# Four small loads from GpSimd to ScalarE's queue, and seven products in the first wide block

## The chip, the cores and the metric

The kernel runs on one core of a Trainium2 chip. The core's engines work side by side, each through its own queue in order: TensorE (PE: matmuls, with PEld its weight loads), VectorE (DVE), ScalarE (ACT), GpSimd (POOL) and SyncE (SP), which here only issues transfers. Three of them issue DMAs: SyncE, ScalarE and GpSimd. The metric is the time on the device in microseconds (us), lower is better.

## What is computed

One layer of a decoder for 256 positions of width 2048, all in float32: a norm, one large projection of 17408 columns, windowed attention in three groups of heads, a gated linear recurrence, gates, a mixing projection, and a gated feed-forward part. The change lies in the first blocks of the projection and in the loads beside them:

```
a = rmsnorm(h, norm_mix_pre[layer])
proj = a @ w_in[layer]
q_a, k_a, v_a, q_r, f_r, i_r, g_r, gate_a, gate_r = split_columns(proj)
...
qh = rotary(heads(q_a), S)                                  # cs: the rotary table
lower_bounds = cumsum(softmax(hgrn_lower_bounds, axis=0), axis=0)
r_out = r_out * hgrn_norm_gain[layer] ... * silu(g_r)       # gainr
y = sigmoid(gate_a) * (attn @ w_attn_branch[layer]) + sigmoid(gate_r) * (r_out @ w_hgrn_branch[layer])
...
a = rmsnorm(h, norm_ffn_pre[layer])
```

## The kernel before

Each float32 matrix is split into a rounded high part and the rest, and a product is made of three matmuls (high x high, high x low, low x high). The split of a weight tile is one copy on ScalarE (the high part, L293 or L328) and one subtraction on VectorE (the rest, L294 or L330).

The weights come in blocks. A block has a number of steps, and each step loads a tile `raw`, splits it and multiplies it. Tiles are loaded about three units ahead (`N_RAW`), splits are written two steps ahead of their matmuls (`AHEAD`), and the split tiles rotate through three buffers (`N_SPLIT`). The order of the work on each engine is the order in which the program writes it; the main loop at the end writes, for each step, the split of the step after next, the load behind that, the step's matmuls, and a piece of whatever stands in the lists `evacs`, `turns` and `lanes`.

The kernel begins with two "N" blocks of eight steps (columns `COL_GR`, the gate of the recurrence, 512 columns each), which accumulate in four banks called `acc`. While the first of them runs, TensorE transposes x (`transpose_in`, L492), ScalarE and VectorE store the transposed x with its high and low parts (L499, L503), and ScalarE squares x for the norm (`sumsq`, L570). A generator `opening` writes these squares, one per step, and behind them the scale of the norm, its broadcast, the rotary tables (`cs`) and the bounds of the recurrence (`rowg`). Between the fourth and the fifth square it writes four loads on GpSimd's queue: `gainr` (the norm's gain broadcast to 128 partitions, 512 KB), two times 16 rows of `rowg` (8 KB each) and `cs` (256 KB). GpSimd has nothing ahead of them but a few fills. When an "N" block is done, `evac_g` empties its two banks: a sigmoid on ScalarE (L747), two products on VectorE (L749 reads the bank, L752 multiplies by `gainr`), and a store.

Behind them stand eight wide blocks (`early`), each 1024 columns in two groups of 512, in eight steps of 256 rows. A plain step multiplies a 2 x 2 arrangement of tiles with eight products, 24 matmuls; its split is L328 and L330. A step "by seven" makes the same contribution with seven products of sums of tiles, 21 matmuls; its split makes sums first (VectorE L334, L340, L341), then high parts (ScalarE L339, L342, L345) and the rest (VectorE L346, L348). It needs sums of the tiles of xT too, which `pair_sums` makes ahead (`x7`, the tiles `so`). The results of a wide block lie in four banks for the pairs (side, group), and the products by seven use four more, `p1`, `p6`, `p5` and `p7`, which `gather` adds behind the last step by seven and `evac_kept` adds to the first four. One kind of bank is called `aux`, the other `acc`; blocks take turns. In the first wide block the pairs lie in `aux`.

The order of a wide block's steps is a list of pairs (tile of rows, by seven or not):

```
FIRST = [(m, 0) for m in range(8)]
EIGHT = [(3, 0), (4, 0), (0, 1), (5, 0), (1, 1), (6, 0), (2, 1), (7, 0)]
```

`FIRST` is used for the first wide block, `EIGHT` for all others. The second wide block begins with a flush of `lanes[1]`, which writes what is left of `pair_sums`. A flush of `evacs` comes behind the second step of each wide block (`turn=1`); in the first wide block it writes what is left of `evac_g` of the second "N" block.

Of the kernel before, what the change touches and what calls it, by code (L numbers as in the profile page):

```python
# [19 lines left out]
P = 128  # L20
# [6 lines left out]
HW = 1024  # L27
# [6 lines left out]
COL_GA, COL_GB = 13312, 15360  # L34

X7 = H7 = (0, 1, 2)
FIRST = [(m, 0) for m in range(8)]
EIGHT = [(3, 0), (4, 0), (0, 1), (5, 0), (1, 1), (6, 0), (2, 1), (7, 0)]
DOWN = [[(m, m in by7) for m in range(KF // 2)] for by7 in (range(4, 20, 3), range(3, 19, 3))]

# [50 lines left out]
def tile_hybrid_block(ctx: ExitStack, tc: tile.TileContext, t, out):  # L91
    nc = tc.nc
# [20 lines left out]
    def hslot(s):  # L113
        return hpool.tile([P, 2, 512], F32, tag="h", bufs=4, name=nm(s))

    def aux():
        return auxp.tile([P, 512], F32, tag="aux", name=nm("aux"))
# [10 lines left out]
    def small(s, n=8, bufs=6):  # L128
        return cpool.tile([P, n], F32, tag=f"small{n}", bufs=bufs, name=nm(s))
# [4 lines left out]
    def rsqrt_mean(dst, ss, n, bias=None):  # L134

        w = ss.shape[-1]
        v, y, a = (small(s)[:, :w] for s in ("v", "y", "a"))  # L140
        bias = bias or (eps[:, 0:1], eps[:, 1:2])
        nc.scalar.activation(y, ss, AF.Ln, scale=1.0 / n, bias=bias[0])
        nc.scalar.activation(y, y, AF.Exp, scale=-0.5)
        nc.vector.tensor_scalar(v, ss, -0.5 / n, bias[1], op0=OP.mult, op1=OP.add)
        if w == 1:
            nc.vector.scalar_tensor_tensor(out=a, in0=y, scalar=v, in1=y, op0=OP.mult, op1=OP.mult)
        else:
            nc.vector.tensor_mul(a, y, y)
            nc.vector.tensor_mul(a, a, v)
        nc.vector.scalar_tensor_tensor(  # L150
            out=dst, in0=a, scalar=1.5, in1=y, op0=OP.add, op1=OP.mult
        )
# [11 lines left out]
    rowg = cpool.tile([48, P], F32, name="rowg")  # L164
# [30 lines left out]
    def ptile(s):  # L195
        n = {"early": 4, "middle": 5, "late": 2}[pool["name"]]
        return pool["now"].tile([P, 512], F32, tag="p", bufs=n, name=nm(s))

    cs = kp.tile([P, 2, S], F32, name="cs")
    amask = kp.tile([P, 2, 512], F32, name="amask")  # L200
    lmask = kp.tile([P, len(LEVELS), 64], F32, name="lmask")
    gainr = kp.tile([P, HW], F32, name="gainr")
# [16 lines left out]
    def add_seven(*args, flip, **kw):  # L219
        b = Wide(*args, **kw)  # L220
        b.flip = flip
        blocks.append(b)
        for i in range(b.steps):
            seq.append(Step(b, i, len(units), 0))
            units.append([seq[-1]])
# [286 lines left out]
    def row_broadcast(dst, rc):  # L512

        ds = [small("diag", P, 2) for _ in range(2)]
        for b in range(2):
            nc.vector.tensor_scalar(ds[b], ident, rc[:, b : b + 1], None, op0=OP.mult)
        yield
        ps = aux()
        for b in range(2):
            mm(ps[:, b * P : (b + 1) * P], ones[:, :P], ds[b], True, True)  # L520
        yield
        nc.scalar.activation(dst, ps[:, :S], AF.Copy)
# [12 lines left out]
    evacs, turns, lanes, work, done = deque(), deque(), [deque(), deque()], deque(), []  # L535
    ready = set()

    def advance(q):
        if q:
            try:  # L540
                next(q[0])
            except StopIteration:
                q.popleft()
                return
# [7 lines left out]
    def flush(q):  # L552
        while q:
            advance(q)


    xt = [hslot("x") for _ in range(4)]
# [3 lines left out]
    xT = Split("xT", KD)  # L561
# [4 lines left out]
    def sumsq(dst, pieces, first=0):  # L566
        for j, x in enumerate(pieces, first):
            for b in range(2):
                junk = ptile("junk")
                nc.scalar.activation(  # L570
                    junk, x[:, b, :], AF.Square, accum_out=dst[:, 4 * b + j : 4 * b + j + 1]
                )
                yield

    def add_parts(dst, ss):
        nc.vector.tensor_reduce(
            dst, ss.rearrange("p (b j) -> p b j", b=2), op=OP.add, axis=mybir.AxisListType.X
        )

    def opening():  # L580
        ss, s2 = small("ss"), small("s2")
        yield from sumsq(ss, xt[:2])
        nc.gpsimd.dma_start(gainr, t["hgrn_norm_gain"].to_broadcast([P, HW]))
        nc.gpsimd.dma_start(rowg[0:16], t["norm_ffn_pre"][0].rearrange("(a p) -> a p", p=P))
        nc.gpsimd.dma_start(
            rowg[16:32], t["hgrn_lower_bounds"].rearrange("l (a p) -> (l a) p", p=P)
        )
        nc.gpsimd.dma_start(cs, t["rope"])
        yield from sumsq(ss, xt[2:], 2)
        add_parts(s2[:, :2], ss)  # L590
        rsqrt_mean(r1c, s2[:, :2], D)
        ready.add("r1c")
        yield from row_broadcast(rowb, r1c)
        ready.add("rowb")
        yield
        for i, (j, c) in enumerate(((0, -QSCALE), (1, -QSCALE), (0, 1.0), (1, 1.0))):
            nc.vector.scalar_tensor_tensor(
                out=tabs[:, i, :].rearrange("p (two j) -> p two j", two=2),
                in0=cs[:, j, :].rearrange("p (j two) -> p two j", two=2), scalar=c,
                in1=rowb.rearrange("p (two j) -> p two j", two=2), op0=OP.mult, op1=OP.mult,  # L600
            )
        yield
        ps = aux()
        nc.tensor.transpose(ps[:, :32], rowg[:32], ident[:32, :32])
        yield
        nc.vector.tensor_copy(colg[:, 16:48], ps[:, :32])
        l0, l1 = colg[:, 32:40], colg[:, 40:48]
        m, e0, e1 = small("m"), small("e0"), small("e1")
        nc.vector.tensor_max(m, l0, l1)
        nc.vector.tensor_sub(e0, l0, m)  # L610
        nc.vector.tensor_sub(e1, l1, m)
        nc.scalar.activation(e0, e0, AF.Exp)
        nc.scalar.activation(e1, e1, AF.Exp)
        nc.vector.tensor_add(e1, e0, e1)
        nc.vector.reciprocal(e1, e1)
        nc.vector.tensor_mul(lb, e0, e1)
        nc.vector.tensor_scalar(lb1, lb, -1.0, 1.0, op0=OP.mult, op1=OP.add)
        ready.add("lb")
        yield
        nc.sync.dma_start(amask, t["amask"])  # L620
        nc.sync.dma_start(lmask, t["lmask"])
# [7 lines left out]
    def start():  # L629
        keep_warm(WARM)  # L630
        ps = aux()
        nc.tensor.transpose(ps[:, :16], rowg[:16], ident[:16, :16])
        nc.vector.tensor_copy(colg[:, :16], ps[:, :16])
        high, low = transpose_in(xt, colg, xT, 0, True)
        for kk in range(2):
            high(kk)
            low(kk)
            split(seq[0], kk)
        keep_warm(BRIDGE - 1)
        split(seq[1])  # L640
        lanes[0].append(opening())

    x7 = {}
# [20 lines left out]
    def evac_kept(key, fn):  # L664
        def go(b):
            dst = keep(key, 1024)
            for s, g in ((0, 0), (0, 1), (1, 0), (1, 1)):
                src = b.bank[s, g]
                if b.rest:
                    e = b.rest[s, g]  # L670
                    nc.vector.tensor_add(e, src, e)
                    src = e
                else:
                    e = eslot()
                nc.scalar.activation(e, src, fn, scale=r1c[:, s : s + 1])
                nc.scalar.dma_start(dst[:, s, g * 512 : (g + 1) * 512], e)
            yield
        return go
# [596 lines left out]
    w_in = t["w_in"][0]  # L1275
# [19 lines left out]
             (COL_GA + 1024, ("a", 1), AF.Sigmoid), (COL_GB + 1024, ("r", 1), AF.Sigmoid)]  # L1295
    early += [(COL_V + 1024 * g, ("v", g), AF.Copy) for g in range(3)] + [(COL_IR, "i", AF.Copy)]
    for n, (col, key, fn) in enumerate(early):
        add_seven(w_in, (col, col + 512), EIGHT if n else FIRST, xT, lambda m: x7[m],
                  evac_kept(key, fn), flip=n % 2 == 1, turn=1,
                  pre=(lambda: flush(lanes[1])) if n == 1 else None)  # L1300
    for half in range(2):
        add_wide(w_in, KD, COL_FR + 512 * half, xT, evac_f(half))
        if half == 0:
# [15 lines left out]
    for j in range(4):  # L1319
        add("N", t["w_mix_out"][0], KD, 512 * j, lambda k: yT[0].after(turns)(k), evac_mix(j),  # L1320
            pre=begin_mix if j == 0 else None)
# [3 lines left out]
        pre=begin_ffn, mid=mid_ffn, post=more_h)  # L1325
    add("N", w, KD, FF, lambda k: hT[0](k), evac_first_up)
    for j in range(1, 11):
        add_seven(w, (512 * j, FF + 512 * j), EIGHT, lambda k: hT[0](k),
                  lambda m: h7[m], evac_ffn, flip=j % 2 == 0, turn=1,
                  pre=(lambda: (flush(evacs), flush(lanes[1]))) if j == 1 else None)  # L1330
    for j in range(2):
        add_seven(t["w_ffn_down"][0], (1024 * j, 1024 * j + 512), DOWN[j], act,
                  lambda m: a7[m], evac_down, prep=prep_act, flip=j == 1,
                  pre=begin_down if j == 0 else None, turn=3 if j == 0 else None)
# [45 lines left out]
    a, b, c = seq[-3:]  # L1380
# [61 lines left out]
```

## Time and profile before

| | us |
|---|---|
| median of three runs | 1722.15 |
| lowest, highest | 1721.54, 1722.41 |
| the profiled execution | 1722.01 |
| its span in the trace | 1720.2 |
| TensorE busy | 1704.2 |
| VectorE busy | 1356.5 |
| ScalarE busy | 895.5 |

Times in the trace count from the start of the span. A row of the timeline has start, length, engine, line, operation, tiles and count; the brackets at its end show how long the engine was idle ahead of it and what ended that. A row of a stretch has for each engine the busy time with the number of instructions, then the granted clock of TensorE, the busy share of the 16 DMA engines, and GB/s. A matmul's length in the trace overlaps the next one's; their pace is read from a row with many of them.

### The profile page before, as it was taken

How to read it: one execution, taken by the hardware profiler on the slowest of the kernel's cores; microseconds unless marked ns; L12 is line 12 of the kernel's file. 1: busy time of each engine (PE TensorE's matmuls, PEld its weight loads, DVE VectorE, ACT ScalarE, POOL GpSimd, SP SyncE). 2: the span in 40 equal slices, each digit the busy share in tenths (PEclk: the TensorE clock that was granted, in tenths of full speed). 3: DMA queues.
4: the chain of work that ended last, by engine and by line, in shares of the span. 5: the costliest groups of instructions: out<-in, count | busy, mean ns of one | idle time of the engine just before them, and what ended most of it. 6: DMA issues, size and time to landing. Idle time of an engine off the chain costs nothing.

```text
span 1720.2 us, 21535 instructions
## 1 busy us (share of the span) xinstructions
PE 1704.2 (99%) x8356; PEld 1431.0 (83%) x8356; DVE 1356.5 (79%) x1477; ACT 895.5 (52%) x1007; POOL 23.7 (1%) x42
## 2 busy tenths in 40 slices
PE   8999999999999999999999999999999999999997
PEld 6888888888888898888888878888888888888886
DVE  5768888886677887777665578888888888898998
ACT  5645555554434434544444466555555555665663
POOL 0000000000000000000000000000000000000000
PEclk9999999999999999999999999999999999999999
DMA  6865666667554655465555745555555555656653
GB/s 241 277 220 209 234 232 226 220 220 257 175 167 160 218 162 172 163 208 168 171 172 188 253 165 202 196 195 196 198 201 202 202 201 200 219 198 215 201 198 115
DMA packets 208678, 344.78 MB, mean 200 GB/s; under 512 B 10960, under 2 KB 77696, under 8 KB 208576
## 3 DMA queue, kind: packets, MB, share of 16 engines
q1 hardware_dynamic: 198496, 318.61, 54.9%
q10 hardware_dynamic: 6880, 13.51, 2.1%
q0 software_dynamic: 3200, 11.29, 2.0%
q8 instruction: 65, 1.06, 0.3%
q14 instruction: 37, 0.30, 0.1%
HBM read 331.83 MB, written 11.53 MB: 200 GB/s over the span
## 4 chain that ended last, share of the span: by engine, by line
PE 97%; DMA 1%; DVE 1%; ACT 0%; SPq 0%; issue 0%; DVEq 0%; ACTq 0%
PE acc L132 63%; PE aux L132 33%; DMA raw<-in_w_in 1%; PE aux L819 0%; DMA gpost<-in_norm_mix_post 0%; PE aux L492 0%; PE acc L1133 0%; DVE fz L1262 0%; PE aux L1133 0%; PE aux L480 0%; ACT junk L1216 0%; DVE e L1212 0%; SPq L564 0%; PE aux L967 0%; SPq L272 0%
## 5 line engine op out<-in xcount | busy, mean ns | idle before, releaser
L294 DVE TENSOR_TENSOR w<-raw,w 128x1024 fp32r<-128x1024 f32 (+1 forms) x225 | 274.2, 1219 | 192.7 <-ACT w L293 192.0
L293 ACT ACTIVATE w<-raw 128x1024 fp32r<-128x1024 f32 (+1 forms) x225 | 236.9, 1054 | 297.3 <-PE acc L132 246.3
L132 PE MATMUL acc<-xT,w 128*128 128x256 f32 (+1 forms) x2048 | 370.4, 339 | 0.0
L132 PEld LDWEIGHTS acc<-xT,w 128*128 128x128 f32 x2048 | 311.6, 188 | 43.3
L330 DVE TENSOR_TENSOR wl<-raw,w 128x2048 fp32r<-128x2048 f32 x125 | 285.9, 2287 | 60.9 <-ACT w L328 60.9
L328 ACT ACTIVATE w<-raw 128x2048 fp32r<-128x2048 f32 x125 | 238.8, 1910 | 132.5 <-PE aux L132 64.2
L346 DVE TENSOR_TENSOR wl<-sum,w 128x2048 fp32r<-128x2048 f32 x63 | 144.3, 2291 | 65.6 <-ACT w L342 65.5
L132 PE MATMUL acc<-w,hT 128*128 128x512 f32 x622 | 181.5, 391 | 0.3 <-ACT hT L499 0.3
L132 PE MATMUL acc<-w,xT 128*128 128x512 f32 x536 | 158.4, 397 | 3.5 <-ACT xT L499 1.9
L339 ACT ACTIVATE w<-sum 128x1024 fp32r<-128x1024 f32 x63 | 67.0, 1063 | 172.5 <-DVE sum L334 153.7
L132 PEld LDWEIGHTS acc<-w,hT 128*128 128x128 f32 x622 | 115.9, 188 | 24.7 <-ACT hT L499 0.5
L132 PE MATMUL aux<-w,hT 128*128 128x512 f32 x430 | 135.6, 389 | 0.0
L132 PEld LDWEIGHTS acc<-w,xT 128*128 128x128 f32 x536 | 101.3, 191 | 26.5 <-ACT xT L499 2.1
L132 PE MATMUL aux<-w,xT 128*128 128x512 f32 x386 | 120.9, 389 | 0.0
L348 DVE TENSOR_TENSOR dl<-raw,dh 128x1536 fp32r<-128x1536 f32 x63 | 110.4, 1752 | 0.0
L132 PEld LDWEIGHTS aux<-w,hT 128*128 128x128 f32 x430 | 80.7, 188 | 16.8
L345 ACT ACTIVATE dh<-raw 128x1536 fp32r<-128x1536 f32 x63 | 92.9, 1474 | 0.0
L132 PE MATMUL acc<-w,yT 128*128 128x512 f32 x384 | 88.2, 390 | 0.1
L132 PEld LDWEIGHTS aux<-w,xT 128*128 128x128 f32 x386 | 72.5, 188 | 15.0
L132 PEld LDWEIGHTS acc<-w,yT 128*128 128x128 f32 x384 | 71.8, 188 | 15.3 <-DVE w L294 0.5
L132 PE MATMUL aux<-wl,hT 128*128 128x512 f32 x215 | 83.6, 389 | 0.0
L132 PE MATMUL acc<-wl,hT 128*128 128x512 f32 x215 | 83.6, 389 | 0.0
(262 smaller groups left out, 2653.9 us busy)
## 6 DMA issues: line engine op xcount, KB each, us to landing
raw<-in_w_in SPq DMA_DIRECT2D x271, 512.0 KB, 4.6
raw<-in_w_ffn_gate_up SPq DMA_DIRECT2D x176, 512.0 KB, 4.4
raw<-in_w_ffn_down SPq DMA_DIRECT2D x88, 512.0 KB, 4.8
raw<-in_w_mix_out SPq DMA_DIRECT2D x32, 512.0 KB, 4.9
kept<-e ACTq DMA_DIRECT2D x32, 256.0 KB, 4.4
raw<-in_w_hgrn_branch SPq DMA_DIRECT2D x16, 512.0 KB, 4.5
raw<-in_w_attn_branch SPq DMA_DIRECT2D x16, 512.0 KB, 4.6
v<-kept POOLq DMA_DIRECT2D x8, 512.0 KB, 6.6
```

Of the source, the lines that this page charges most:

```text
L132: nc.tensor.matmul(ps, lhsT, rhs, start=start, stop=stop, skip_group_check=True)
L293: nc.scalar.activation(wh[:, k], raw[:, k], AF.Copy)
L294: nc.vector.tensor_sub(wl[:, k], raw[:, k], wh[:, k].bitcast(F32))
L328: nc.scalar.activation(hi, raw, AF.Copy)
L330: nc.vector.tensor_sub(lo, raw, hi.bitcast(F32))
L339: nc.scalar.activation(hi[:, :1024], s[:, :1024], AF.Copy)
L345: nc.scalar.activation(dhi, d, AF.Copy)
L346: nc.vector.tensor_sub(lo, s, hi.bitcast(F32))
L348: nc.vector.tensor_sub(dlo, d, dhi.bitcast(F32))
```

## The change

The four loads are written on ScalarE's queue, behind six squares instead of four. The first wide block takes the list `EIGHT` as the others do, so that its third, fifth and seventh steps go by seven, and it gathers; the flush of `lanes[1]` moves from the second wide block to the first. One line falls away, so the lines of the changed kernel are one lower.

```diff
-FIRST = [(m, 0) for m in range(8)]
 EIGHT = [(3, 0), (4, 0), (0, 1), (5, 0), (1, 1), (6, 0), (2, 1), (7, 0)]
...
         ss, s2 = small("ss"), small("s2")
-        yield from sumsq(ss, xt[:2])
-        nc.gpsimd.dma_start(gainr, t["hgrn_norm_gain"].to_broadcast([P, HW]))
-        nc.gpsimd.dma_start(rowg[0:16], t["norm_ffn_pre"][0].rearrange("(a p) -> a p", p=P))
-        nc.gpsimd.dma_start(
+        yield from sumsq(ss, xt[:3])
+        nc.scalar.dma_start(gainr, t["hgrn_norm_gain"].to_broadcast([P, HW]))
+        nc.scalar.dma_start(rowg[0:16], t["norm_ffn_pre"][0].rearrange("(a p) -> a p", p=P))
+        nc.scalar.dma_start(
             rowg[16:32], t["hgrn_lower_bounds"].rearrange("l (a p) -> (l a) p", p=P)
         )
-        nc.gpsimd.dma_start(cs, t["rope"])
-        yield from sumsq(ss, xt[2:], 2)
+        nc.scalar.dma_start(cs, t["rope"])
+        yield from sumsq(ss, xt[3:], 3)
...
-        add_seven(w_in, (col, col + 512), EIGHT if n else FIRST, xT, lambda m: x7[m],
+        add_seven(w_in, (col, col + 512), EIGHT, xT, lambda m: x7[m],
                   evac_kept(key, fn), flip=n % 2 == 1, turn=1,
-                  pre=(lambda: flush(lanes[1])) if n == 1 else None)
+                  pre=(lambda: flush(lanes[1])) if n == 0 else None)
```

The order on the engines: on ScalarE, in the eighth step of the first "N" block, where `w` is a split weight tile, `x` and `junk` belong to the squares:

```order
L570 ACTIVATE junk_356,ss_213<-x_112 128x512
L293 ACTIVATE w_358<-raw_179 128x1024 [waits DMAHW7_49,DVE_49]
L570 ACTIVATE junk_375,ss_213<-x_113 128x512 [waits DMAHW4_49]
L293 ACTIVATE w_385<-raw_179 128x1024 [waits DMAHW0_49,DVE_49,PE_49]
L570 ACTIVATE junk_401,ss_213<-x_113 128x512 [waits Activation_49]
L411 ACTIVATE so_379<-s_380 128x512 [waits DVE_49]
```

With the change:

```order
L569 ACTIVATE junk_352,ss_213<-x_112 128x512
L292 ACTIVATE w_354<-raw_179 128x1024 [waits DMAHW7_49,DVE_49]
L582 DMA gainr<-in_hgrn_norm_gain 128x1024
L583 DMA rowg<-in_norm_ffn_pre 16x128
L584 DMA rowg<-in_hgrn_lower_bounds 16x128
L587 DMA cs<-in_rope 128x512 [waits DMAHW0_49]
L569 ACTIVATE junk_375,ss_213<-x_113 128x512 [waits DMAHW4_49]
L292 ACTIVATE w_385<-raw_179 128x1024 [waits DVE_49,PE_49]
```

The four loads have moved between the sixth and the seventh square, and the last of them waits for an earlier DMA (DMAHW0 is one of the counters of completed transfers). On VectorE, at the splits for the first wide block (`wl` is the rest of a weight tile, `sig` the gate in work, `g` its result):

```order
L330 TENSOR_TENSOR wl_596<-raw_472,w_595 128x2048
L413 TENSOR_TENSOR so_567<-s_568,so_567 128x512
L330 TENSOR_TENSOR wl_616<-raw_517,w_615 128x2048
L330 TENSOR_TENSOR wl_655<-raw_577,w_654 128x2048
L749 SCALAR_TENSOR_TENSOR sig_652<-acc_410,r1c,sig_652 128x512
L752 TENSOR_TENSOR g_650<-sig_652,gainr 128x512
```

With the change:

```order
L329 TENSOR_TENSOR wl_596<-raw_472,w_595 128x2048
L412 TENSOR_TENSOR so_567<-s_568,so_567 128x512
L333 TENSOR_TENSOR sum_617<-raw_517 128x1024
L339 TENSOR_TENSOR sum_617<-raw_517,sum_617 128x512
L340 TENSOR_TENSOR sum_617<-raw_517,sum_617 128x512
L345 TENSOR_TENSOR wl_616<-sum_617,w_615 128x2048
L347 TENSOR_TENSOR dl_624<-raw_517,dh_623 128x1536
L329 TENSOR_TENSOR wl_664<-raw_577,w_663 128x2048
L748 SCALAR_TENSOR_TENSOR sig_661<-acc_410,r1c,sig_661 128x512
L751 TENSOR_TENSOR g_659<-sig_661,gainr 128x512
```

Five instructions stand in the place of one, ahead of the reading of the bank `acc_410`.

On TensorE, in the third step of the first wide block, before (the first of its four banks, `aux_622`, and the start of the second; `w` and `wl` are the two parts of the weights):

```order
L132 MATMUL aux_622<-w_615,xT_116 128x512 [waits Activation_49]
L132 MATMUL aux_622<-wl_616,xT_116 128x512 [waits DVE_49]
L132 MATMUL aux_622<-w_615,xT_116 128x512 x2
L132 MATMUL aux_622<-wl_616,xT_116 128x512
L132 MATMUL aux_622<-w_615,xT_116 128x512
L132 MATMUL aux_629<-w_615,xT_116 128x512
```

With the change, the products `p6`, `p5` and `p7`, which have three matmuls each in banks of the kind `acc`:

```order
L131 MATMUL acc_728<-w_615,so_379 128x512
L131 MATMUL acc_728<-wl_616,so_379 128x512
L131 MATMUL acc_728<-w_615,so_379 128x512
L131 MATMUL acc_732<-w_615,so_379 128x512 [waits DVE_49]
L131 MATMUL acc_732<-wl_616,so_379 128x512
L131 MATMUL acc_732<-w_615,so_379 128x512
L131 MATMUL acc_736<-w_615,so_379 128x512 [waits DVE_49]
L131 MATMUL acc_736<-wl_616,so_379 128x512
L131 MATMUL acc_736<-w_615,so_379 128x512
```

The step has taken on banks that the second "N" block used, and waits for VectorE ahead of two of them.

## Prediction

> **What bounds the kernel now.** I read the page first, then stretches of the opening by engine, then the timeline and the chain of waits up to the end of the first wide block.
>
> ```profile
> PE 1704.2 (99%) x8356; PEld 1431.0 (83%) x8356; DVE 1356.5 (79%) x1477; ACT 895.5 (52%) x1007; POOL 23.7 (1%) x42
> PE 97%; DMA 1%; DVE 1%; ACT 0%; SPq 0%; issue 0%; DVEq 0%; ACTq 0%
> ```
>
> TensorE carries 97% of the chain that ended last. So a change counts where TensorE waits, where its clock is low, or by the matmuls that it takes away. The waits lie in the opening, and so does a slow clock:
>
> ```profile
> core 0: us, PE busy (x) PEld busy (x) DVE busy (x) ACT busy (x) POOL busy (x), PEclk, DMA share, GB/s
> 2.00:4.00 2.00, 2.00 (x6) 0.76 (x5) 0.00 (x0) 0.46 (x1) 0.24 (x1) 1.00 0.87 243
> 4.00:6.50 2.50, 2.50 (x13) 1.20 (x11) 0.91 (x3) 1.27 (x3) 1.37 (x3) 1.00 0.92 270
> 7.81:11.23 3.42, 2.15 (x10) 1.61 (x11) 0.69 (x1) 0.87 (x2) 0.00 (x0) 1.00 1.05 386
> 11.23:14.64 3.41, 1.55 (x8) 0.81 (x7) 1.23 (x1) 1.05 (x2) 0.00 (x0) 1.00 1.04 390
> 14.64:18.06 3.42, 2.11 (x4) 1.29 (x5) 2.56 (x5) 3.42 (x8) 0.00 (x0) 0.50 1.05 386
> 18.06:21.47 3.41, 3.41 (x9) 2.58 (x9) 1.46 (x2) 0.42 (x1) 0.00 (x0) 0.50 1.05 386
> 21.47:24.90 3.43, 3.43 (x19) 2.78 (x18) 1.15 (x3) 2.40 (x5) 0.00 (x0) 1.00 1.05 385
> ```
>
> The DMA engines are full (share 1.04 to 1.06) while TensorE is idle for half of 11.23 to 14.64. Behind that idle stretch the granted clock is 0.50 for 6.83 us. The chain there, in order of time (start, length, what):
>
> ```profile
> 4.57 9.82 DMA raw<-in_w_in
> 14.41 1.06 ACT w L293
> 17.18 4.54 PE acc L132 x10
> 22.15 2.78 PE acc L132 x12
> 63.07 43.80 PE aux L132 x192
> ```
>
> A weight load issued at 4.57 lands at 14.39; ScalarE, in order, splits it (L293) before it can take xT (L499), and only then TensorE goes on. The last row is the first wide block: TensorE without a gap. The same place in the timeline (start, length, what, and in brackets the idle time ahead and what ended it):
>
> ```profile
> 1.55 0.69 POOL L583 DMA_DIRECT2D gainr<-in_hgrn_norm_gain  x1
> 6.12 0.57 POOL L588 DMA_DIRECT2D cs<-in_rope  x1
> 8.18 0.63 ACT L293 ACTIVATE w<-raw 128x512 fp32r<-128x512 f32 x1 [1.59 <-DMA raw<-in_w_in]
> 10.51 1.64 PE L132 MATMUL acc<-w,xT 128*128 128x512 f32 x6
> 13.38 0.63 PE L492 MATMUL aux<-ident,x 128*128 128x128 f32 x4 [1.23 <-DMA x<-in_x]
> 15.88 5.83 PE L132 MATMUL acc<-w,xT 128*128 128x512 f32 x12 [1.88 <-ACT xT L499]
> ```
>
> TensorE ends the first step at 12.15 and has only four transposes (0.63) to do before it resumes at 15.88. ScalarE waited for weights already at 8.18.
>
> **The four loads leave the opening: gain.** GpSimd issues gainr (512 KB), two loads of 8 KB and cs (256 KB) between 1.55 and 6.69 us, into the full stretch. Up to the landing at 14.39 the queues moved (packets, MB, share; q0 is GpSimd's, q1 SyncE's), and from 4.0 to 6.5 (last two rows):
>
> ```profile
> q1 hardware_dynamic: 1929, 3.18, 63.8%
> q0 software_dynamic: 288, 0.80, 17.9%
> ...
> q0 software_dynamic: 131, 0.50, 70.6%
> q1 hardware_dynamic: 103, 0.17, 21.2%
> ```
>
> Lower bound: 0.80 MB less at 0.390 MB per us is 2.05 us. Upper bound: from 4.0 to 6.5 the engines moved only 270 GB/s, most of it gainr; if q1 alone ran at 388 from 4.0 on, its remaining 2.7 MB (3.18 less the 2 us at 243 before) would be in at 10.95, 3.4 us earlier. I take 3.0, nearer the upper end, since the slow stretch coincides with gainr's packets. The resumption follows the landing: 15.88 becomes 12.9.
>
> The clock adds to that. The first step ends at 12.15 now because the second half of its weights is split at 8.18; ScalarE is free for that 1.59 earlier, so the step would end near 10.6. The gap to 12.9 holds 0.6 us of transposes, so 1.7 us are idle. In 3.41 us that leaves 1.7 busy, between the 1.55 after which the clock fell and the 2.15 after which it did not. I take it that the clock holds (about 2 in 3). Then the ten matmuls of 4.54 us take 10 x 2.78 / 12 = 2.3: 2.2 us less. Gain of the opening: 3.0 + 2.2 = 5.2 us; bounds 2.05 and 5.6.
>
> **ScalarE issues them: nothing, while covered.** On ScalarE's queue (the order above) the issues stand ahead of the last two squares, behind a weight split. What such issues cost on this queue, and what waits there:
>
> ```profile
> 36.33 1.05 ACT L293 ACTIVATE w<-raw 128x1024 fp32r<-128x1024 f32 x1
> 37.28 0.62 ACT L570 ACTIVATE junk<-x 128x512 f32<-128x512 f32 x1
> 40.34 0.63 ACT L411 ACTIVATE so<-s 128x512 fp32r<-128x512 f32 x1 [0.78 <-DVE s L409]
> 50.21 0.69 DVE L752 TENSOR_TENSOR g<-sig,gainr 128x512 f32<-128x512 f32 x1
> ...
> 940.23 3.24 ACTq L1017 DMA_DIRECT2D hx<-in_x  x4
> ...
> 1480.83 0.83 ACTq L1185 DMA_DIRECT2D fpost<-in_norm_ffn_post  x2
> ```
>
> fpost is a broadcast like gainr, 0.41 us each, and starts while the ACTIVATE ahead of it runs. Four take 1.65 from 36.34 on, so the square moves from 37.28 to 38.0. That 0.7 vanishes in the 0.78 for which L411 waits on VectorE anyway. At hx's 0.81 each (3.24) the delay would be 2.3, 1.5 past the cover, on VectorE's path; four 128- and 16-row transfers are nearer fpost. cs's issue waits (DMAHW0 in the order) for an earlier DMA of SyncE, the weights that the split after the square needs landed in any case. GpSimd's queue loses four issues and next waits for g at 50 us. Nothing waits for the data: gainr is first read at 50.21, over 10 us behind the issue, and SyncE's weight loads of 30 to 40 us do not fill the engines.
>
> **The first wide block: 9 matmuls less, 3.3 us of waits more.** A step has 24 matmuls, by seven products 21. At 43.80 / 192 = 0.228 us, three such steps save 2.05. Against that stands VectorE's order: the long split of step 2 (steps counted from 0; L333 to L347 with the change) now stands ahead of L748, which empties the bank acc_410, and TensorE's order shows that the fifth product (acc_732) and the seventh (acc_736) wait for VectorE, since they take over the two banks of the second "N" block.
>
> Durations, VectorE first: the next block's split by seven products, then what stands there now; ScalarE behind it.
>
> ```profile
> 66.30 2.29 DVE L330 TENSOR_TENSOR wl<-raw,w 128x2048 fp32r<-128x2048 f32 x1
> 72.98 0.75 DVE L749 SCALAR_TENSOR_TENSOR sig<-acc,r1c,sig 128x512 f32<-128x512 f32 x1
> 75.15 0.69 DVE L752 TENSOR_TENSOR g<-sig,gainr 128x512 f32<-128x512 f32 x1
> ...
> 116.51 1.22 DVE L334 TENSOR_TENSOR sum<-raw 128x1024 f32<-128x1024 f32 x1
> 122.52 1.76 DVE L348 TENSOR_TENSOR dl<-raw,dh 128x1536 fp32r<-128x1536 f32 x1
> ```
>
> ```profile
> 65.35 1.28 ACT L747 ACT_TABLE_LOAD   x1
> 66.65 0.69 ACT L747 ACTIVATE sig<-acc,r1c 128x512 f32<-128x512 f32 x1
> 74.27 1.92 ACT L328 ACTIVATE w<-raw 128x2048 fp32r<-128x2048 f32 x1 [2.95 <-PE aux L132]
> ...
> 120.18 1.47 ACT L345 ACTIVATE dh<-raw 128x1536 fp32r<-128x1536 f32 x1
> ```
>
> Such a split takes 124.28 - 116.51 = 7.77 us. In today's times (the gain of the opening shifts everything alike, since these engines follow TensorE's steps up to 35 us): it runs 66.3 to 74.07, and TensorE, done with step 1 at 74.2 (the release of L328), starts step 2 unhindered. ScalarE: L345 until 71.4, table 72.7, sigmoid 73.3, L328 of step 3 until 75.2. VectorE: L330 until 77.5, then the first bank at 78.2; the second at 79.55. The fifth product comes at 74.2 + 12 x 0.228 = 76.9 and waits 1.3; the seventh waits another 0.65. Step 2 ends at 80.95, step 3 at 86.4. Step 4's split starts when both gates are done (72.98 to 75.84 is 2.86), at 80.2, and ends at 87.97; its second matmul, due at 86.6, waits 1.35. Step 6's split begins at 90.2 and ends at 97.95, when TensorE arrives: no wait. Together 3.3 - 2.05 = 1.25 us longer. This end hangs on VectorE alone; were the banks free and the splits early, it would be 2.05 shorter.
>
> The steps' weights come in another order, in loads of the same size, and the flush moved to this block finds only work that stood in the same place (L412). The gather and four additions behind the block cost VectorE more, but the second block carries them today without a wait of TensorE.
>
> **Sum.** 1722.01 (the profiled execution; the median is 0.14 above) - 5.2 + 1.25 = 1718.1.
>
> **Rivals.** (1) The clock falls again. The gap is close to the one that made it fall; then only the landing counts: 1722.0 - 3.0 + 1.25 = 1720.3, or 1721.2 with 2.05. The Trainium skill (TensorE: Matmul & The Clock Gate, the HAM clock gate) says the windows of 3.4 us run freely, so that the loss varies between executions of one kernel. That agrees with 6.83 us here being two windows; one execution can't show the varying. (2) The block doesn't wait: 1722.0 - 5.2 - 2.05 = 1714.8. Against it stands the order above. (3) Slower: the opening gains nothing, because q1's pace is set by something other than q0, and ScalarE's issues cost hx's price: 1722.0 + 1.25 + 1.5 = 1724.8; it is slower than before once the opening gives under 1.25 us (2.75 with the dear issues). The 21.2% against 70.6% speaks against it. By the Trainium skill (DMA: Bandwidth & Descriptors, Rules for kernel authors) spreading DMAs over issuing engines doesn't help, as all share 16 engines; by that alone the opening gives 0. The trace agrees on the sharing, but here the time of issue moves too.
>
> **Numbers.** Forecast 0.50, rival (1) 0.25, (2) 0.13, (3) 0.08, other 0.04. A measurement of this kernel tells some 0.2% (3.4 us) from no change, so the borders are 1718.7 and 1725.6. The forecast's own range, 1716.8 to 1719.7 (landing 2.05 to 3.4, block 0.8 to 2), lies two thirds below 1718.7: 0.34; with (2), 0.01 of (1) and half of the others, faster has 0.50. Same has 0.44: 0.16 of the forecast, 0.24 of (1), half of (3). Slower by over 0.2% has 0.06: the other half of (3), which 1724.8 lies close to, and half of the others. The range from 1715.0 to 1721.9 leaves out half of (2) and all of (3).
>
> **What would show it.** Right: no q0 before 14 us, the weight load of 4.57 landing at 11 to 12, clock 1.00 to 21 us, the second step's ten matmuls in 2.3 us; in the first wide block waits of TensorE of about 1.3 and 0.65 in step 2 and 1.35 in step 4. Wrong: a stretch of clock 0.50 behind the opening, L411 later against the transposes than now, or no wait for L748's banks.

## The result, and the profile after

| us | before | after |
|---|---|---|
| median of 20 executions each | 1721.49 | 1720.43 |
| lowest, highest | 1720.95, 1722.89 | 1718.82, 1722.49 |
| the profiled execution | 1722.01 | 1718.82 |
| its span | 1720.2 | 1717.0 |

The ratio is 0.9992, interval 0.9985 to 0.9999: faster by 0.08%, inside the 0.2% that count as no change. The profiled execution of after is the lowest of its twenty, and it gained 3.2 us, three times what the medians gained. So two questions stand: do the parts of the sum show in this profile, and what do the other executions lose again?

The profile's busy times of after (engine, us, share, instructions): TensorE has the nine instructions less.

```profile
PE 1700.6 (99%) x8347; PEld 1428.2 (83%) x8347; DVE 1373.6 (80%) x1497; ACT 900.3 (52%) x1014; POOL 21.7 (1%) x38
```

The chain of waits of after (start, length, what):

```profile
4.38 7.17 DMA raw<-in_w_in
...
14.34 2.60 PE acc L131 x10
17.38 2.78 PE acc L131 x12
...
97.67 6.12 PE aux L131 x27
103.79 12.24 PE acc L131 x54
```

The load lands at 11.55 instead of 14.39, 2.84 earlier. The ten matmuls take 2.60 instead of 4.54, and the step behind them starts at 17.38 instead of 22.15: the opening gained 4.77. The first wide block ends at 103.79; before, at 63.07 + 43.80 = 106.87. So 3.08 of the 4.77 are left, and the block itself became 1.69 longer.

The opening by stretches, in the columns of the table shown of before (the last three numbers are the granted clock, the DMA share and GB/s):

```profile
4.00:6.50 2.50, 2.50 (x10) 1.37 (x9) 0.51 (x2) 0.84 (x2) 0.00 (x0) 1.00 0.89 262
11.23:14.64 3.41, 1.23 (x5) 0.59 (x4) 1.97 (x4) 3.06 (x8) 0.00 (x0) 1.00 1.05 387
14.64:18.06 3.42, 3.42 (x18) 2.78 (x17) 2.05 (x4) 1.66 (x4) 0.00 (x0) 1.00 1.05 386
18.06:21.47 3.41, 3.41 (x19) 2.79 (x18) 2.10 (x3) 2.59 (x7) 0.00 (x0) 1.00 1.06 389
```

The clock is 1.00 throughout. From 4.0 to 6.5 the DMA engines moved 262 GB/s without GpSimd's loads, 270 with them; what changed is whose bytes they are, SyncE's alone now:

```profile
q1 hardware_dynamic: 477, 0.65, 89.2%
```

0.65 MB against 0.17. ScalarE's timeline around the four issues (its queue is ACTq):

```profile
30.32 0.36 ACTq L582 DMA_DIRECT2D gainr<-in_hgrn_norm_gain  x1
30.71 0.46 ACTq L583 DMA_DIRECT2D rowg<-in_norm_ffn_pre  x1
31.20 0.44 ACTq L584 DMA_DIRECT2D rowg<-in_hgrn_lower_bounds  x1
31.68 0.43 ACTq L587 DMA_DIRECT2D cs<-in_rope  x1
32.53 0.62 ACT L569 ACTIVATE junk<-x 128x512 f32<-128x512 f32 x1
35.58 0.63 ACT L410 ACTIVATE so<-s 128x512 fp32r<-128x512 f32 x1 [0.78 <-DVE s L408]
```

The square stands at 32.53 where 37.28 less 4.77 puts it, and the 0.78 that L410 waits for VectorE is untouched. Nothing was pushed back.

In the first wide block, TensorE and VectorE in the timeline:

```profile
71.79 0.39 PE L131 MATMUL acc<-w,so 128*128 128x512 f32 x1
73.52 0.50 PE L131 MATMUL acc<-w,so 128*128 128x512 f32 x1 [1.35 <-DVE sig L748]
73.86 0.40 PE L131 MATMUL acc<-wl,so 128*128 128x512 f32 x1
74.10 0.39 PE L131 MATMUL acc<-w,so 128*128 128x512 f32 x1
74.91 0.50 PE L131 MATMUL acc<-w,so 128*128 128x512 f32 x1 [0.43 <-DVE sig L748]
75.25 0.39 PE L131 MATMUL acc<-wl,so 128*128 128x512 f32 x1
...
81.85 0.39 PE L131 MATMUL aux<-dh,xT 128*128 128x512 f32 x1
83.32 0.50 PE L131 MATMUL aux<-dl,xT 128*128 128x512 f32 x1 [1.08 <-DVE dl L347]
83.65 0.39 PE L131 MATMUL aux<-dh,xT 128*128 128x512 f32 x1
```

```profile
70.52 2.29 DVE L329 TENSOR_TENSOR wl<-raw,w 128x2048 fp32r<-128x2048 f32 x1 [1.22 <-ACT w L327]
72.73 0.74 DVE L748 SCALAR_TENSOR_TENSOR sig<-acc,r1c,sig 128x512 f32<-128x512 f32 x1
74.11 0.74 DVE L748 SCALAR_TENSOR_TENSOR sig<-acc,r1c,sig 128x512 f32<-128x512 f32 x1
75.50 1.22 DVE L333 TENSOR_TENSOR sum<-raw 128x1024 f32<-128x1024 f32 x1
81.51 1.75 DVE L347 TENSOR_TENSOR dl<-raw,dh 128x1536 fp32r<-128x1536 f32 x1
```

TensorE waits three times where the block had no gap: twice for the banks that L748 empties, once for step 4's `dl`. The clock stays at 1.00 behind the banks here:

```profile
76.00:79.50 3.50, 3.50 (x17) 2.90 (x16) 2.30 (x4) 2.35 (x3) 1.14 (x2) 1.00 0.94 311
```

The executions of after, sorted by the mean granted clock listed with each: eight at 0.999 took 1718.82 to 1719.61 us, ten at 0.996 to 0.998 took 1720.34 to 1721.06, two at 0.995 took 1722.28 and 1722.49. A stretch of 3.41 us at half clock (half of the 6.83 us seen in the profile of before) lowers the mean over 1717 us by 3.41 x 0.5 / 1717 = 0.001 and costs up to 1.7 us of matmuls. By the times, then, the ten look as if they had one such stretch more and the two as if they had two. The means alone would allow one to four; they are rounded, and they also count the end of the kernel, where no matmul runs (clock 0.61 from 1712 to 1715 us in the profile of after). Theory: the parts of the sum came as in the profile, and the clock, kept there, falls in most executions. Rivals: the block's waits alone cost more than the profile shows, or the loads gain less.

### The profile page after: what moved, and what is told of

Read it like the earlier page. It is cut to its first block, busy times and chain, and to the rows that moved or that the text cites. A ratio compares the mean times of both kernels' runs of the same rounds, so it can differ in the third digit from the quotient of the medians.

```text
span 1717.0 us, 21554 instructions
## 1 busy us (share of the span) xinstructions
PE 1700.6 (99%) x8347; PEld 1428.2 (83%) x8347; DVE 1373.6 (80%) x1497; ACT 900.3 (52%) x1014; POOL 21.7 (1%) x38
## 3 DMA queue, kind: packets, MB, share of 16 engines
q8 instruction: 65, 1.06, 0.3%
## 4 chain that ended last, share of the span: by engine, by line
PE 94%; DVE 3%; ACT 1%; DMA 1%; issue 1%; SPq 0%; ACTq 0%; DVEq 0%
PE acc L131 62%; PE aux L131 31%; DVE w L293 1%; DMA raw<-in_w_in 0%; PE aux L818 0%; DMA gpost<-in_norm_mix_post 0%; PE aux L491 0%; PE acc L1132 0%; DVE fz L1261 0%; PE aux L1132 0%; ACT w L327 0%; PE aux L479 0%; ACT junk L1215 0%; ACT w L292 0%; DVE sig L748 0%
## 5 line engine op out<-in xcount | busy, mean ns | idle before, releaser
L329 DVE TENSOR_TENSOR wl<-raw,w 128x2048 fp32r<-128x2048 f32 x122 | 279.0, 2286 | 41.6 <-ACT w L327 41.5
L327 ACT ACTIVATE w<-raw 128x2048 fp32r<-128x2048 f32 x122 | 232.9, 1909 | 110.1 <-PE aux L131 43.9
L345 DVE TENSOR_TENSOR wl<-sum,w 128x2048 fp32r<-128x2048 f32 x66 | 151.2, 2291 | 68.9 <-ACT w L341 68.8
L347 DVE TENSOR_TENSOR dl<-raw,dh 128x1536 fp32r<-128x1536 f32 x66 | 115.6, 1751 | 0.0
L131 PE MATMUL aux<-w,xT 128*128 128x512 f32 x344 | 108.5, 389 | 0.0
L344 ACT ACTIVATE dh<-raw 128x1536 fp32r<-128x1536 f32 x66 | 97.3, 1474 | 0.0
L131 PE MATMUL acc<-w,a 128*128 128x512 f32 x268 | 83.7, 389 | 0.0
```

The lines of the kernel that those rows point to most:

```text
L131: nc.tensor.matmul(ps, lhsT, rhs, start=start, stop=stop, skip_group_check=True)
L327: nc.scalar.activation(hi, raw, AF.Copy)
L329: nc.vector.tensor_sub(lo, raw, hi.bitcast(F32))
L344: nc.scalar.activation(dhi, d, AF.Copy)
L345: nc.vector.tensor_sub(lo, s, hi.bitcast(F32))
L347: nc.vector.tensor_sub(dlo, d, dhi.bitcast(F32))
```

## The experiments

Before was run again beside each of the three batches of experiments, with medians of 1721.54 us (the loads alone, the block alone and the two first bridges), 1721.36 (steps 3 and 5 with and without the bridge, the loads late on GpSimd, the banks first) and 1721.26 (the rest). A difference between versions of different batches carries these 0.3 us. Behind each median stand in brackets the lowest and the highest execution, then the ratio to before and its 95% interval.

**The loads alone.** The first wide block stays as before.

```diff
+FIRST = [(m, 0) for m in range(8)]
...
-        add_seven(w_in, (col, col + 512), EIGHT, xT, lambda m: x7[m],
+        add_seven(w_in, (col, col + 512), EIGHT if n else FIRST, xT, lambda m: x7[m],
                   evac_kept(key, fn), flip=n % 2 == 1, turn=1,
-                  pre=(lambda: flush(lanes[1])) if n == 0 else None)
+                  pre=(lambda: flush(lanes[1])) if n == 1 else None)
```

> The change's loads alone: four loads on ScalarE behind six squares, the first wide block plain as before. Theory (the opening gives some 4.8 us in an execution whose clock holds, and the block by seven takes back 1.7): about 1.7 us faster than the change, median near 1718.7, and no wait of TensorE in the first wide block beyond 0.4 us. Rival (the block's waits are made good later, so its 9 matmuls less do count): about 2 us slower than the change, near 1722.5.

Measured: 1718.67 us (1716.99 to 1719.62; ratio 0.9982, interval 0.9974 to 0.9991). The block has no wait. The median's gain is 2.9 against 1721.54, well short of the profile's 4.77.

**The block alone.** The four loads stay on GpSimd's queue.

```diff
-        yield from sumsq(ss, xt[:3])
-        nc.scalar.dma_start(gainr, t["hgrn_norm_gain"].to_broadcast([P, HW]))
...
+        yield from sumsq(ss, xt[:2])
+        nc.gpsimd.dma_start(gainr, t["hgrn_norm_gain"].to_broadcast([P, HW]))
```

> The change's wide block alone, the loads on GpSimd as before. Theory: three waits of about 1.3, 0.65 and 1.35 us in the block against 2.05 saved, so 1.3 to 1.7 us slower than the kernel before, near 1723. Rival: the block saves its 9 matmuls, 2 us faster, near 1719.5.

Measured: 1723.97 us (1722.65 to 1724.87; ratio 1.0013, interval 1.0004 to 1.0022), 2.4 longer than before, more than the 1.69 of the profile and than the 1.3 to 1.7 expected. Its profiled execution is its highest, 1724.87; its timeline and its stretches show a cause:

```profile
79.14 0.50 PE L132 MATMUL acc<-w,so 128*128 128x512 f32 x1 [1.35 <-DVE sig L749]
80.52 0.50 PE L132 MATMUL acc<-w,so 128*128 128x512 f32 x1 [0.42 <-DVE sig L749]
```

```profile
75.00:79.50 4.50, 3.15 (x15) 2.33 (x14) 3.34 (x3) 1.67 (x2) 0.00 (x0) 1.00 0.73 233
79.50:83.00 3.50, 3.08 (x10) 2.15 (x9) 3.43 (x5) 0.56 (x1) 1.68 (x3) 0.75 0.93 322
83.00:87.00 4.00, 4.00 (x15) 3.19 (x14) 2.84 (x3) 3.69 (x4) 0.15 (x1) 0.79 0.73 242
```

Behind the two waits the granted clock falls a second time, here in the block. In the profile of after the same waits left it at 1.00. In all the profiles of this document the clock is 1.00 from 1.5 to 1700 us outside two places, the opening (14.6 to 25 us) and the first wide block (72 to 95 us).

**A bridge over the gap of the opening.** `keep_warm(n)` is a function that the kernel already has: n products on a tile of zeros into a bank whose result nothing uses. Here six of them stand behind the transposes at which TensorE waits in the opening, in the change and, as seven, in the kernel before.

```diff
             transpose_in(xt, colg, xT, c + 2)
+            if c == 0:
+                keep_warm(6)
```

> The change, with six matmuls on zeros between the third group of transposes and the second step of the opening, where TensorE is idle for 1.6 us. Theory (executions of the change differ by whether the granted clock falls behind that gap): the spread of 3.7 us shrinks under 1 us, all near the fastest, median near 1719.2, and clock 0.998 or more in all. Rival (the spread has another cause, such as the transfers): median near 1720.4 and spread as before.

> The kernel before with seven such matmuls at the same place, where it is idle for 1.9 us. Theory: the clock stays up behind the gap, ten matmuls that took 4.54 us take 2.6, so 1.5 to 2 us faster than the kernel before, near 1719.8, with a spread under 1 us. Rival (the clock isn't what this costs): the same as before within 0.5 us.

Measured: the change with the bridge 1719.21 us (1718.57 to 1720.27; ratio 0.9986, interval 0.9977 to 0.9995), 1.2 less than the change. Before with the bridge 1719.73 (1719.33 to 1720.18; ratio 0.999, interval 0.9981 to 0.9998), 1.8 less than before. In the chain of waits of the latter the load lands at 14.22, as late as ever, but the ten matmuls are fast:

```profile
4.77 9.45 DMA raw<-in_w_in
...
17.00 2.56 PE acc L132 x10
```

So the loss of clock in the opening is worth 1.8 us in the median by itself, with no load moved. The bridged change has the median expected, but should have lain within 1 us and spread over 1.7. Its profiled execution is its highest, 1720.27, and shows where, again behind the waits for the banks (at 74.50 and 75.89):

```profile
76.00:79.40 3.40, 3.40 (x9) 2.63 (x10) 3.08 (x4) 1.28 (x2) 1.27 (x3) 0.51 1.02 398
```

**The loads alone with the bridge.** The same six products in the kernel with the loads alone.

> The moved loads alone, the first wide block as before, with six products on zeros in the opening's gap. Theory: what is left of the spread of the moved loads alone (1716.99 to 1719.62 us) is the opening's clock; with it kept, the median is 1717.1 us and the executions lie within 1.0 us. The version with products by seven at steps 3 and 5 and the same bridge ran at 1715.93, so those two products would be worth 1.2. Rival: the clock falls elsewhere, and the median stays at 1718.0 or more.

Measured: 1717.41 us (1717.0 to 1717.77; ratio 0.9977, interval 0.9968 to 0.9986), where 1717.1 was expected. With no wait in the block and a bridge in the opening, the spread falls from 2.6 to 0.8. That gives the parts with the clock kept and as they ran:

| median, us | loads as before | loads moved | loads moved, block changed |
|---|---|---|---|
| without bridge | 1721.49 | 1718.67 | 1720.43 |
| with bridge | 1719.73 | 1717.41 | 1719.21 |

The landing is worth 2.3 (second row); the loads as they ran 2.8; the block costs 1.8 in both rows. With each version taken against before of its own batch, the landing is worth 2.0 and the block costs 1.8 and 1.5: the sizes hold to some 0.3 us.

The loads alone, and the version of the next paragraph, have the same opening without a bridge, and there the same gap had two outcomes. The first matmul that ends the gap, and the ten behind it (timeline, then chain), for the loads alone:

```profile
13.86 0.73 PE L132 MATMUL acc<-w,xT 128*128 128x512 f32 x2 [2.08 <-ACT xT L499]
```

```profile
15.15 2.56 PE acc L132 x10
```

and for the version with products by seven at steps 3 and 5:

```profile
13.57 0.73 PE L132 MATMUL acc<-w,xT 128*128 128x512 f32 x2 [2.09 <-ACT xT L499]
```

```profile
14.86 3.87 PE acc L132 x10
```

2.08 us of idle kept the clock, 2.09 lost it: the length of the gap alone doesn't decide.

**Products by seven at steps 3 and 5.** The block takes two steps by seven instead of three, the fourth and the sixth (3 and 5 counted from 0) instead of the third, fifth and seventh, with the change's loads; then the same with the bridge.

```diff
+FIRST = [(3, 0), (4, 0), (5, 0), (0, 1), (6, 0), (1, 1), (2, 0), (7, 0)]
...
-        add_seven(w_in, (col, col + 512), EIGHT, xT, lambda m: x7[m],
+        add_seven(w_in, (col, col + 512), EIGHT if n else FIRST, xT, lambda m: x7[m],
```

> The change, with the first wide block's order such that only its fourth and sixth steps go by seven (tiles 3, 4, 5, 0 by seven, 6, 1 by seven, 2, 7). Theory (what the block costs are the waits, because VectorE comes too late with the split of the third step): by the durations of the change VectorE is ready for both steps, no wait over 0.4 us, 6 matmuls less than plain, so 3 us faster than the change, median near 1717.4. Rival (any step by seven in this block costs its gain): no faster than the loads alone, 1718.7 or more.

> The same with six matmuls on zeros in the gap of the opening. If both theories hold: median near 1716.2 and a spread under 1 us. If the clock's rival holds: as without them.

Measured: 1717.01 us (1715.59 to 1718.64; ratio 0.9975, interval 0.9965 to 0.9984), and with the bridge 1715.93 (1715.72 to 1716.49; ratio 0.9969, interval 0.9958 to 0.9981), both as expected. TensorE has no wait in the block. Against the loads alone with the bridge the two steps gain 1.48; six matmuls at 0.228 are 1.37. Products by seven in this block save what they should once the banks are free.

**A late issue on GpSimd's queue.** The change with the four loads back on GpSimd's queue, held there by a copy that waits for the sixth square.

```diff
+    eps2 = cpool.tile([P, 1], F32, name="eps2")
...
         yield from sumsq(ss, xt[:3])
-        nc.scalar.dma_start(gainr, t["hgrn_norm_gain"].to_broadcast([P, HW]))
+        nc.gpsimd.tensor_copy(eps2, ss[:, 6:7])
+        nc.gpsimd.dma_start(gainr, t["hgrn_norm_gain"].to_broadcast([P, HW]))
...
```

> The change, but the four loads are issued by GpSimd, which waits for the sixth square first (a copy of one column of the sums). Theory (the time of the issue counts, not the engine): within 0.5 us of the change, and the weight load issued at 4.4 lands at 11.5. Rival (ScalarE as the issuing engine is what helps): the landing goes back towards 14.4 and the time to that of the kernel before or worse.

Measured: 1720.8 us (1719.2 to 1722.34; ratio 0.9996, interval 0.9987 to 1.0005), 0.4 from the change. The load of 4.40 landed at 12.17, though all four loads are GpSimd's (issued from 33.97 us on, ScalarE's in the change from 30.32):

```profile
4.40 7.77 DMA raw<-in_w_in
...
14.95 4.08 PE acc L131 x10
```

What counts here is when they are issued, not by which engine: the block alone, whose loads GpSimd issues early, ran at 1723.97 with the landing at 14.39. The ten matmuls of 4.08 show that in this execution, whose opening and block are those of the change, the clock fell in the opening; behind the waits of the block it stayed at 1.00. The Trainium skill (DMA: Bandwidth & Descriptors, Rules for kernel authors) says of the engines that choosing among them gives no bandwidth; this pair agrees.

**The banks first.** In the change, `evac_g`'s flush stands behind the block's first step instead of its second, so L748 reads the banks ahead of step 3's split.

```diff
-                  evac_kept(key, fn), flip=n % 2 == 1, turn=1,
+                  evac_kept(key, fn), flip=n % 2 == 1, turn=1 if n else 0,
```

> The change, with the flush that empties the banks behind the first step of the first wide block instead of the second, so that the banks come free ahead of the split of the fourth step. Theory (the end of the block hangs on VectorE's splits, not on the banks): the two waits for banks of 1.3 and 0.5 us vanish, but the fifth step then waits about 2 us for its split, and the sum gains at most 1 us on the change. Rival (the banks are the cause): the change gains 1.8 us or more.

Measured: 1717.93 us (1717.33 to 1719.83; ratio 0.9981, interval 0.9972 to 0.999), 2.5 less than the change, where at most 1 was expected and the rival said 1.8 or more. The waits for the banks are gone, and the one for `dl` grew to the 2 us expected, at a clock that stayed at 1.00; then VectorE's timeline:

```profile
81.94 0.50 PE L131 MATMUL aux<-dl,xT 128*128 128x512 f32 x1 [1.94 <-DVE dl L347]
```

```profile
83.00:87.00 4.00, 4.00 (x19) 3.33 (x18) 3.60 (x4) 1.36 (x2) 0.00 (x0) 1.00 0.91 315
```

```profile
69.14 0.74 DVE L748 SCALAR_TENSOR_TENSOR sig<-acc,r1c,sig 128x512 f32<-128x512 f32 x1
71.92 2.28 DVE L329 TENSOR_TENSOR wl<-raw,w 128x2048 fp32r<-128x2048 f32 x1
74.12 1.22 DVE L333 TENSOR_TENSOR sum<-raw 128x1024 f32<-128x1024 f32 x1
80.13 1.75 DVE L347 TENSOR_TENSOR dl<-raw,dh 128x1536 fp32r<-128x1536 f32 x1
```

The 1.22 us for which L329 waited on ScalarE in the change are now filled with L748 and L751, so step 4's split starts at 74.12 instead of 75.50 and `dl` is done 1.38 earlier. That accounts for 1.4 (the spans are 1717.0 and 1715.6, both with the opening's clock kept); the expectation had left VectorE's idle time out. The other 1.1 of the medians would go with a clock that falls less often: seven of eleven executions lie within 0.7 us at the low end. Where the clock fell in the other four isn't shown.

**The banks first, with the bridge.** Both edits in the change.

> The change, with six products on zeros in the opening's gap and with step 2's pair of banks taken first in the first wide block. Theory: with the opening's clock kept, the executions still differ because the two waits at the banks of the products by seven (1.35 and 0.42 us) let the clock fall behind them in some. Those waits are gone here and one wait of about 1.9 us for dl is left, so the median is 1717.4 us and the executions lie within 1.0 us. Rival: the waits at the banks have no part in it, and the executions keep the 1.7 us of spread and a median of 1718.5 or more; the remaining wait of 1.9 us would then be enough to make the clock fall.

Measured: 1717.94 us (1717.52 to 1720.44; ratio 0.998, interval 0.9971 to 0.9989), no less than without the bridge (1717.93), while the bridge took off 1.1 to 1.8 us in the four other pairs. Why it gives nothing here stays open. The median of 1717.4 and the spread of 1 us were missed: eight executions lie from 1717.52 to 1718.35, the other three at 1718.87, 1719.63 and 1720.44. The profiled one is the highest, and behind the one wait that is left, for `dl`, the clock is half:

```profile
82.53 0.50 PE L131 MATMUL aux<-dl,xT 128*128 128x512 f32 x1 [1.90 <-DVE dl L347]
```

```profile
83.00:86.40 3.40, 3.40 (x10) 2.61 (x9) 3.37 (x3) 0.47 (x1) 0.00 (x0) 0.50 0.77 246
```

So the waits at the banks aren't special: the one wait of 1.90 us was followed by a stretch at half clock too, though the wait of 1.94 us in the profile without the bridge was not. That much of the rival came; its median of 1718.5 did not.

**Steps 3 and 5, bridge and banks first.** All three edits together.

> The version with products by seven at steps 3 and 5 and the bridge, with step 2's pair of banks taken first as well. Theory: TensorE waits at no bank there, so the banks' order has nothing to give: 1715.9 us, within 0.4 of the version without it. Rival: VectorE, which no longer waits for ScalarE's evictions, prepares the later steps earlier, as it did in the change with the banks' order alone: 1714.7.

Measured: 1715.80 us (1715.14 to 1716.62; ratio 0.9969, interval 0.9957 to 0.998), 0.1 from the version without the banks' order, as expected. Where TensorE doesn't wait, an earlier VectorE gives nothing. These two versions are 5.4 and 5.5 us, 0.31%, faster than before, and some 4.5 us faster than the change.

## Why the prediction was right or wrong

The range (1715.0 to 1721.9) holds 1720.43, and the outcome is "within 0.2%", which had 0.44; the time is 2.3 us above the 1718.1 forecast, which lies below all twenty executions, beside rival (1), the clock falling again at 1720.3. That rival's sum meets the time by luck: its landing is 0.7 to 1.0 too large and its start 0.5 too high (one profiled execution, 1722.01, for a median of 1721.49), against a clock term of nothing that should be 0.5 to 0.8 and a block 0.3 to 0.6 too cheap.

**Landing: right in kind, too large by 0.7 to 1.0.** 3.0 was taken; the profile of after gained 2.84, the bridged pair of medians 2.3, or 2.0 against before of their own batches. Over the ten profiles here with the loads moved the load lands between 11.55 and 12.55, the profile of after being the earliest, 12.02 on the average; with them in the opening it lands at 14.22 to 14.39, 14.33 on the average of three. That is 2.3 again. 0.2 of it comes ahead of the load: SyncE issues it at 4.38 instead of 4.57. The upper bound rested on gainr's packets slowing the stretch from 4.0 to 6.5. They don't: SyncE's own loads ran at 262 GB/s there. The gain fits the lower bound's way of counting, bytes taken out of the way (2.05 for 0.80 MB, and the 0.2 of the earlier issue).

**The clock: the step that failed.** "I take it that the clock holds (about 2 in 3). Then the ten matmuls of 4.54 us take 10 x 2.78 / 12 = 2.3: 2.2 us less." In the profile it held and the ten took 2.60. Over the executions it did not hold often enough, as the bridges show. Kept by a bridge, it is worth 1.8 in the median (before with the bridge) and not 2.2, and of that 1.26 is still to be had once the loads are moved (1718.67 to 1717.41; 1.0 against before of each batch): the moved loads saved 0.5 to 0.8 in the median. A single outcome was put into the sum where 1721.49 is the median of a mixture. The working did weigh busy shares of one window, 1.55 against 2.15, but the same 3.41 us in other profiles don't bear that border out: the clock kept with 1.23 us busy in the profile of after (its row stands above), and with 1.28 in that of the loads alone:

```profile
11.23:14.64 3.41, 1.28 (x6) 0.60 (x6) 1.94 (x3) 2.25 (x5) 0.00 (x0) 1.00 1.04 383
```

The Trainium skill (TensorE: Matmul & The Clock Gate, the HAM clock gate), cited for rival (1), says that the windows run freely. The two gaps of 2.08 and 2.09 with different outcomes, and stretches of some 3.4 us at half clock, agree with it. Why the clock holds in one execution and not in another was not measured.

**The block: right to 0.1 us on VectorE, and 0.44 too cheap on TensorE.** With 4.77 subtracted, the working has the first bank free at 73.43, the second at 74.78, step 4's split from 75.43 to 83.20. The rows above give 73.47, 74.85, 75.50 and 83.26. The waits, from when the matmul was due, are 1.50, 0.58 and 1.24, together 3.32 for the 3.3 predicted (due: 0.23 after the start of the matmul ahead, 71.79, 74.10 and 81.85). The block came out 1.69 longer instead of 1.25. Most of the difference is the restart: the matmul behind each wait takes 0.33 to 0.34 to the next start (73.52 to 73.86, 74.91 to 75.25, 83.32 to 83.65) where 0.23 is the pace, some 0.33 for three.

**What the block's waits do to the clock was not in the sum.** The profiles of the block alone (2.4 longer), of the bridged change (spread over 1.7) and of the banks first with the bridge have the clock lowered behind these waits, down to half; that this is all of the 0.7 by which the block alone exceeds 1.69 isn't shown. The prediction asked of one gap only, in the opening, whether it makes the clock fall; it made three more, two of them 1.4 us apart.

**"This end hangs on VectorE alone": only half right.** Banks first shows that the 1.22 us in which VectorE waited for ScalarE's L327, which the working has as 74.07 to 75.2, were time that the order could have used.

**ScalarE's issues at nothing: right.** 0.36 to 0.46 each, as fpost's 0.41 said. They start at 30.32, 1.25 ahead of the 36.34 - 4.77 taken, beside the ACTIVATEs ahead of them, so that not even the 0.7 of delay came that L410's wait was to cover. The rivals "the block doesn't wait" (1714.8) and "slower" (1724.8) are refuted by the waits and by the landing.

Against the profiled executions, then, the sum is -2.84 (landing), -1.93 (clock), +1.69 (block): -3.08 of -3.19. In medians it is -2.3 (landing), -0.5 (clock), +1.8 (block). That these give the measured -1.06 proves nothing, since the three are differences between the same medians; against before of each batch they are -2.0, -0.8 and +1.8.

## What to carry to other kernels

A gain that hangs on the granted clock is a mixture over executions: put the share in which the clock is kept into the sum, and ask of every new wait, not just the one that is being removed, whether it makes the clock fall. Where a gap can't be closed, a few products on zeros in it can keep the clock (1.1 to 1.8 us in four pairs here, nothing in a fifth), and a kernel with a bridge also measures what the clock was worth. Before a step that costs VectorE more is put into a block, look at which banks that engine has yet to empty: two steps by seven, one step later, gained where three cost 1.5 to 1.8 us.

## What was not expected of the hardware

- Waits of 1.35 and 0.42 us, 1.4 us apart, or one of 1.90 to 1.94, were followed by some 3.4 us at half clock in some profiles and by none in others.
- A gap of 2.09 us was followed by about one such stretch in one profile; in the profile of before two (6.83 us) followed idle times of 1.23 and 1.88 us with only four transposes between.
- Without GpSimd's loads the opening still moved only 262 GB/s from 4.0 to 6.5 us, at a DMA share of 0.89, while the rows from 11 us on have 386 to 389.
- The same load in the same opening landed between 11.55 and 12.55 us over ten profiles: a part of what one profiled execution shows varies with the execution.
